# Two quarters of an output weight: split halves stored by one tile and loaded by the next, in a two-layer encoder kernel

## The chip, the cores and the metric

The kernel runs on one core of a Trainium2 chip. The metric is the device time of one execution in microseconds (us); the median of three runs is taken. The engines are TensorE (PE; its weight loads are PEld), VectorE (DVE), ScalarE (ACT), GpSimd (POOL) and SyncE (SP), which issues nearly all transfers.

## The reference

Two layers over 2048 rows of width 1024: a chunked gating mixer, then attention of chunks of 64 rows over a band of nine chunks, whose output is gated, multiplied by `w_out` (1024 x 1024) and added to the residual; a last norm ends it.

```python
def chunk_attention_mixer(h, k_pad, v_pad, w_qz, rel_bias, w_out):
    q, z = jnp.split(h @ w_qz, 2, axis=-1)
    ...
    def one_chunk(args):
        ...
        sc = jnp.einsum('bqhd,bkhd->bhqk', qc, kc).astype(jnp.float32) + bias
        sc = jnp.where(valid[None, None, None, :], sc, NEG_INF)
        p = jax.nn.softmax(sc, axis=-1).astype(vc.dtype)
        return jnp.einsum('bhqk,bkhd->bqhd', p, vc)
    ...
    return (o * jax.nn.silu(z)) @ w_out

def reference(x, ...):
    x = x + gmlp_mixer(rms_norm(x, a_norm_g[0]), ...)      # layer A
    k_pad, v_pad = shared_kv(x, kv_norm_g, w_kv)
    x = x + chunk_attention_mixer(rms_norm(x, b_norm_g[0]), k_pad, v_pad, ...)
    return rms_norm(x, final_norm_g)
```

## The kernel before

All products are made of three matmuls each (`mm3`, L110): a float32 operand is split into a high part, which is its conversion to the TensorE format by ScalarE, and a low part, which is the operand less the high part, by VectorE. `split_in` (L240) does this for a weight block of 128 x 1024: one conversion (L241) and one subtraction (L242).

Layer A and the values of all heads come first. What matters here is the attention layer, whose first load of values (`V`) is issued at 1521.4 us. It goes through four tiles `t` = 0 to 3 of 512 rows, and in each through eight pairs of heads `p`. In a pair, `score` makes the scores of a block of 128 rows (tiles `s`; VectorE takes bias and maximum into `pr`, `nm`; ScalarE the exponential; GpSimd the scaling), `flip` transposes them (`tp`) and splits the result into `pt` (ScalarE L1583, VectorE L1584), and `value` multiplies `pt` with the values (`pv`). There is one buffer each for `s` and for `tp`, so the next one waits until VectorE has read the last. Between these steps TensorE is given other matmuls: the projections of the next pair (`pj`) and the output product of the tile before (`bo`).

The output product of a tile is a Strassen scheme of seven phases in the order `PHS` = 1, 7, 2, 6, 5, 4, 3 with two row groups `jp` each, so 14 products of 12 matmuls. Phase `ph` takes a quarter of `w_out`, or a sum of quarters, as its right side, in two blocks `q` = 0, 1, each as a high and a low half. The right sides of phases 4 to 7 are sums: while tile 1 runs, `o_sums` makes and splits them and stores the halves in DRAM as `ows[ph, q]`; later tiles load the two halves (512 KB each). Phases 1, 2 and 3 take plain quarters (`o_raw`): each tile loads them raw (512 KB per block, tile `raw_bo`) and splits them. For tiles 0, 1 and 2 this is `o_right(t)` with the output product `outs[t]` run while tile t + 1 is attended to; the halves lie in the eight buffers of tag `T`, which the projection weights share. For the last tile it is `last_right(ph, q)`: phases 1, 7, 6 and 4 use tag `T` (`whbo`, `wlbo`), phase 2 the four buffers of tag `raw` (also `whbo`, `wlbo`), phase 5 a buffer of `V`, and phase 3 the one of `PT` (both `wbo`), which is free after the last `value`. The first 13 of its 56 steps run within the last head pair, the rest after it.

`last_open` loads the rest of the left side for the last tile into `A_hh`; `third` forms a difference of it on GpSimd. The rows of the results are called `row0` to `row3` in the last tile and `oc`, `ou` before; finished rows of the third tile are stored to `x2d`, loaded again as `y`, scaled (L1907) and stored to the output.

The program states the dependences; a scheduler puts each engine's instructions in an order, and each engine then works through its own in that order. `on_beat` ties an instruction behind the last transpose of the latest `flip`. An instruction that issues a transfer stands in the order of the engine that issues it, here SP, or ScalarE.

## Time and profile before

| What | Value |
|---|---|
| median of three runs | 2639.57 us (2638.92 to 2641.89) |
| profiled execution | 2640.17 us, its span 2638.1 us |
| granted TensorE clock, mean | 0.999 |
| data moved by transfers | 720.31 MB, mean 273 GB/s |
| 512 KB loads of raw output-weight blocks (`raw_bo`) | 24, 4.4 us to landing in the median |
| 512 KB loads of stored halves (`wh_bo`, `wl_bo`) | 24 each, 5.1 and 6.0 us |

The span is what the profiler saw from the first to the last instruction; the execution's own time lies 2.07 us above it. Times of instructions are counted from the span's start. In the rows of the profile the names have no numbers, so `wl_bo` stands for the low halves of all phases of tiles 0 to 2, and `wlbo` for those of the last tile.

### The profile page before, as it was taken

To read this page: it belongs to the slowest core of one execution; us is meant where nothing else is said; L and a number is where in the kernel's file an instruction comes from. 1 tells how busy PE (TensorE), PEld (TensorE's weight loads), DVE (VectorE), ACT (ScalarE), POOL (GpSimd) and SP (SyncE) were. 2 spreads that over 40 slices of the span, in tenths; PEclk is the share of its full clock that TensorE was granted. 3 is DMA by queue.
4 is the path that set the end of the run, shared out by engine and by line. 5 is a ranking of instruction groups with operands and counts; after the bars stand their busy time and mean duration, and the time that the engine had idled before them with its cause. 6 is when DMAs were issued, how large, how long until landed. Compare 5 with 4: busy or idle time off the path is not lost. (4 is left out here: it accounts for less than half of the span.)

```text
span 2638.1 us, 38018 instructions
## 1 busy us (share of the span) xinstructions
PE 2604.5 (99%) x12976; PEld 2177.8 (83%) x12976; DVE 1871.4 (71%) x2942; ACT 1314.7 (50%) x2331; POOL 890.1 (34%) x871
## 2 busy tenths in 40 slices
PE   9999999999999999999999999999999999999997
PEld 7888888788888888888888878888888888888886
DVE  6655676766667668757776767778778777877677
ACT  6422243443433434343466466666656655666564
POOL 4611335143252332203334334343333322332245
PEclk9999999999999999999999999999999999999999
DMA  7898998999988968968886587778787767775676
GB/s 299 316 345 332 347 364 319 315 327 328 333 302 303 331 224 310 342 205 262 322 279 234 184 277 236 233 244 260 248 278 253 228 208 222 252 228 162 192 229 249
DMA packets 275153, 720.31 MB, mean 273 GB/s; under 512 B 28944, under 2 KB 68880, under 8 KB 274960
## 3 DMA queue, kind: packets, MB, share of 16 engines
q1 hardware_dynamic: 268096, 704.25, 78.1%
q10 hardware_dynamic: 6864, 13.63, 1.4%
q8 instruction: 104, 1.70, 0.3%
q14 instruction: 89, 0.73, 0.1%
HBM read 532.69 MB, written 174.59 MB: 268 GB/s over the span
## 5 line engine op out<-in xcount | busy, mean ns | idle before, releaser
L111 PE MATMUL P<-T,S 128*128 128x512 f32 x1248 | 495.3, 397 | 0.0
L113 PE MATMUL P<-T,S 128*128 128x512 f32 x1248 | 487.6, 391 | 0.1
L112 PE MATMUL P<-T,S 128*128 128x512 f32 x1248 | 487.0, 390 | 0.0
L1563 POOL TENSOR_SCALAR pr<-pr,sl 128x640 f32<-128x640 f32 (+4 forms) x256 | 207.9, 812 | 554.1 <-DVE sl L1562 477.7
L111 PE MATMUL pj<-hh_b,wh_b 128*128 128x512 f32 x768 | 318.6, 415 | 0.0
L113 PE MATMUL pj<-hh_b,wl_b 128*128 128x512 f32 x768 | 304.0, 396 | 0.3 <-DVE wl_b L242 0.2
L112 PE MATMUL pj<-hl_b,wh_b 128*128 128x512 f32 x768 | 302.7, 394 | 0.0
L1559 ACT ACTIVATE pr<-pr,nm 128x640 f32<-128x640 f32 (+4 forms) x256 | 195.6, 764 | 198.8 <-DVE nm L1549 196.6
L113 PEld LDWEIGHTS P<-T,S 128*128 128x128 f32 x1248 | 234.3, 188 | 51.0 <-DVE S L463 0.4
L112 PEld LDWEIGHTS P<-T,S 128*128 128x128 f32 x1248 | 235.0, 188 | 44.7 <-DVE T L463 0.4
L111 PEld LDWEIGHTS P<-T,S 128*128 128x128 f32 x1248 | 234.7, 188 | 44.5 <-issue 0.2
L1584 DVE TENSOR_TENSOR pt<-tp,pt 128x640 fp32r<-128x640 f32 (+4 forms) x256 | 188.7, 737 | 48.9 <-ACT pt L1583 46.0
L1549 DVE CUSTOM_DVE_ANT_0 pr<-s,bias 128x640 f32<-128x640 f32 (+4 forms) x256 | 188.3, 736 | 43.8 <-PE s L1541 38.8
L1583 ACT CAST pt<-tp 128x640 fp32r<-128x640 f32 (+4 forms) x256 | 158.6, 619 | 38.5 <-PE tp L1579 32.6
L1579 PE MATMUL tp<-ident,pr 128*128 128x128 f32 x1120 | 166.5, 274 | 8.5 <-DVE pt L1584 7.4
L113 PEld LDWEIGHTS pj<-hh_b,wl_b 128*128 128x128 f32 x768 | 144.2, 188 | 34.5 <-DVE wl_b L242 2.3
L1579 PEld LDWEIGHTS tp<-ident,pr 128*128 128x128 f32 x1120 | 130.9, 140 | 42.5 <-issue 13.8
L111 PEld LDWEIGHTS pj<-hh_b,wh_b 128*128 128x128 f32 x768 | 145.1, 189 | 17.7 <-ACT wh_b L241 1.2
L1604 PEld LDWEIGHTS pv<-pt,V 128*128 128x128 f32 x896 | 142.8, 188 | 20.3 <-DVE pt L1584 3.4
L112 PEld LDWEIGHTS pj<-hl_b,wh_b 128*128 128x128 f32 x768 | 145.1, 189 | 16.5
L1604 PE MATMUL pv<-pt,V 128*128 128x256 f32 (+3 forms) x896 | 154.8, 320 | 0.8 <-ACT pt L1583 0.5
L242 DVE TENSOR_TENSOR wl_b<-raw_b,wh_b 128x1024 fp32r<-128x1024 f32 x96 | 121.0, 1261 | 25.1 <-ACT wh_b L241 22.9
(307 smaller groups left out, 5720.8 us busy)
## 6 DMA issues: line engine op xcount, KB each, us to landing
S<-hsd SPq DMA_DIRECT2D x288, 512.0 KB, 5.3
rw<-in_w_a SPq DMA_DIRECT2D x108, 512.0 KB, 6.2
raw_b<-wk SPq DMA_DIRECT2D x75, 512.0 KB, 4.5
A<-ytd SPq DMA_DIRECT2D x72, 512.0 KB, 5.7
hsd<-S SPq DMA_DIRECT2D x56, 512.0 KB, 4.9
V<-vhd SPq DMA_DIRECT2D x56, 512.0 KB, 5.6
bias<-reld SPq DMA_DIRECT2D x64, 320.0 KB, 4.0
va<-vd SPq DMA_DIRECT2D x32, 512.0 KB, 5.7
```

The lines of the kernel that those rows point to most:

```text
L111: first = mm(ps, lh, rh, start=first, stop=False)
L112: mm(ps, lh, rl, start=False, stop=False)
L113: mm(ps, ll, rh, start=False, stop=last)
L242: tv(wl[:], raw[:], wh[:].bitcast(F32), op=sub)
L1549: peak = nc.vector.tensor_tensor_reduce(out=pr[:, c0:].rearrange("p (a b) -> p a b", a=nseg), in0=ps[:, :nseg, :w], in1=bias[:, c0:].rearr ...
L1559: nc.scalar.activation(pr[:, c0:], pr[:, c0:], AF.Exp, scale=-1.0, bias=nm[:], accum_out=sl[:])
L1563: nc.gpsimd.tensor_scalar(pr[:, c0:], pr[:, c0:], sl[:], 1.0, op0=ALU.mult, op1=ALU.mult)
L1579: ins = tpose(tp[:, b, :], pr[:, b * P : (b + 1) * P], ident[:])
L1583: nc.scalar.copy(oh, tp[:, b0:5, :].rearrange("p a b -> p (a b)"))
L1584: nc.vector.tensor_tensor(pt[:, 2560 + o + b0 * P : 2560 + o + 640], tp[:, b0:5, :].rearrange("p a b -> p (a b)"), oh.bitcast(F32), op=ALU ...
L1604: mm(po[:, q0 * P : q1 * P], vtl[t, p][:, i, hs], rhs, start=(i == blocks[0] and j == 0), stop=(i == 7 and j == 1),)
```

## The change

The halves of phase 3 that `o_right(1)` splits (while the third tile, t = 2, is attended to) and those of phase 2 that `o_right(2)` splits (while the last tile is attended to) are put on a list `halves_out`. One entry of the list is stored to `ows` behind each `flip`, issued by ScalarE: 8 stores of 512 KB. The third tile's product then loads the halves of phase 3, and the last tile's product those of phases 2 and 3, as it does for phases 4 to 7. Each such block costs two loads of 512 KB where it was one load and a split. Six blocks of 128 x 1024 are concerned. Phase 1 is split as before.

```diff
     ows = {
         (ph, q): dram.tile([P, 2, 1024], F32, name=f"ows{ph}_{q}")
-        for ph in range(4, 8) for q in range(2)
+        for ph in range(2, 8) for q in range(2)
     }
...
                 w = [w_tile(f"w{i}_{name}") for i in "hl"]
-                if ph in o_raw:
+                if ph in o_raw and (t, ph) != (2, 3):
                     raw = raw_w(1, f"raw_{name}")
                     nc.sync.dma_start(raw[:], wb_out[o_raw[ph]][q])
                     hi = split_in(raw, *w)
                     if (ph, q) == (1, 1):
                         on_beat(hi)
+                    if (t, ph) in ((1, 3), (2, 2)):
+                        halves_out.extend(
+                            (ows[ph, q][:, i, :], w[i][:].bitcast(F32)) for i in range(2)
+                        )
                 else:
...
         owed_out = []
+        halves_out = []
...
                 w = [w_tile(f"w{i}{name}")[:] for i in "hl"]
-            if ph in o_raw:
+            if ph == 1:
                 raw = raw_w(NT - 1, f"raw_{name}")
...
                     send_all()
+                    if halves_out:
+                        on_beat(nc.scalar.dma_start(*halves_out.pop(0)))
                     square_all()
```

The scheduler's order moves with it, at the end of the program above all. In the names below, the digits behind a name are tile, phase and block or row group (`wl_bo2_3_0`: third tile, phase 3, block 0), the last tile's names have no tile number, and the last number counts the buffers.

VectorE, in the last tile while heads 13 and 14 are worked on, before (`Slo` are low halves of the left side, `pr`, `nm`, `sl` belong to the scores, `ou` are results of the third tile):

```order
L242 TENSOR_TENSOR wl_bo2_3_0_25169<-raw_bo2_3_0_25170,wh_bo2_3_0_25168 128x1024
L1562 RECIPROCAL sl3_14_1_25136<-sl3_14_1_25136 128x1
L1584 TENSOR_TENSOR pt3_13_25014<-tp3_13_3_25152,pt3_13_25014 128x640
L1957 TENSOR_TENSOR ou2_7_0_23262<-bo2_4_0_25141,ou2_7_0_23262 128x512
L242 TENSOR_TENSOR wl_bo2_3_1_25175<-raw_bo2_3_1_25176,wh_bo2_3_1_25174 128x1024
L1549 ISA pr3_14_2_25191,nm3_14_2_25192<-s3_14_2_25186,bias3_14_24925 128x640
L1549 ISA nm3_14_2_25192 128x1
L361 TENSOR_TENSOR Slo2_3_0_25239<-A2_01_23593,Sho2_3_0_25238 128x512
L1562 RECIPROCAL sl3_14_2_25193<-sl3_14_2_25193 128x1
L1626 TENSOR_TENSOR og32_3_6_25023<-pv3_13_25202,ot3_13_25228 64x512
L1584 TENSOR_TENSOR pt3_14_25219<-tp3_14_0_25220,pt3_14_25219 128x640
L1742 SCALAR_TENSOR_TENSOR A_hh_25180<-og32_3_6_25023,Z3_6_24702 128x256 x2
```

and now:

```order
L1566 RECIPROCAL sl3_14_1_25148<-sl3_14_1_25148 128x1
L1588 TENSOR_TENSOR pt3_13_25026<-tp3_13_3_25164,pt3_13_25026 128x640
L1962 TENSOR_TENSOR ou2_7_0_23270<-bo2_4_0_25153,ou2_7_0_23270 128x512
L1553 ISA pr3_14_2_25199,nm3_14_2_25200<-s3_14_2_25194,bias3_14_24937 128x640
L1553 ISA nm3_14_2_25200 128x1
L365 TENSOR_TENSOR Slo2_3_0_25247<-A2_01_23601,Sho2_3_0_25246 128x512
L1566 RECIPROCAL sl3_14_2_25201<-sl3_14_2_25201 128x1
L1630 TENSOR_TENSOR og32_3_6_25035<-pv3_13_25210,ot3_13_25236 64x512
L1747 SCALAR_TENSOR_TENSOR A_hh_25188<-og32_3_6_25035,Z3_6_24714 128x256 x2
L1588 TENSOR_TENSOR pt3_14_25227<-tp3_14_0_25228,pt3_14_25227 128x640
```

The two subtractions of phase 3 are gone, and the two `A_hh` now stand ahead of the first `pt3_14`.

SyncE, in the last 50 us of the program, before:

```order
L1897 DMA y2_0_1_25507<-x2d2_0_154 128x512
L1787 DMA whbo_6_0_25548<-ows6_0_106 128x1024
L1787 DMA wlbo_6_0_25549<-ows6_0_106 128x1024
L1787 DMA whbo_6_1_25552<-ows6_1_107 128x1024
L1787 DMA wlbo_6_1_25553<-ows6_1_107 128x1024
L1667 DMA out_0<-y2_0_0_25506 128x512
L1667 DMA out_0<-y2_0_1_25507 128x512
L1901 DMA y2_2_25581<-x2d2_2_156 128x1024
L1787 DMA wbo_5_1_25622<-ows5_1_105 128x1024 x2
L1795 DMA row3_25627<-x1d3_63 128x1024
L1787 DMA whbo_4_0_25648<-ows4_0_102 128x1024
L1787 DMA wlbo_4_0_25649<-ows4_0_102 128x1024
```

and now:

```order
L1902 DMA y2_0_1_25511<-x2d2_0_158 128x512
L1792 DMA wbo_5_0_25520<-ows5_0_108 128x1024 x2
L1792 DMA whbo_6_0_25552<-ows6_0_110 128x1024
L1792 DMA wlbo_6_0_25553<-ows6_0_110 128x1024
L1792 DMA whbo_6_1_25556<-ows6_1_111 128x1024
L1792 DMA wlbo_6_1_25557<-ows6_1_111 128x1024
L1672 DMA out_0<-y2_0_0_25510 128x512
L1672 DMA out_0<-y2_0_1_25511 128x512
L1906 DMA y2_2_25585<-x2d2_2_160 128x1024
L1792 DMA wbo_5_1_25626<-ows5_1_109 128x1024 x2
L1800 DMA row1_25629<-x1d3_63 128x1024
L1800 DMA row3_25631<-x1d3_63 128x1024
```

The two loads of `wbo_5_0` and that of `row1`, which stood some 15 to 20 rows further ahead, now stand here; behind these rows come the halves of phase 4 as before, and then four loads of `wbo_3_0` instead of the two raw ones.

VectorE, from the split of the left side of phase 3 in the last tile on, before:

```order
L361 TENSOR_TENSOR Qlo_3_0_25802<-A_hl_25181,Qho_3_0_25801 128x512
L1957 TENSOR_TENSOR row1_25625<-bo_4_0_25794,ou3_7_0_25586 128x512
L1784 TENSOR_TENSOR wbo_3_0_25678<-raw_bo_3_0_25679,wbo_3_0_25678 128x1024
L1784 TENSOR_TENSOR wbo_3_0_25678<-raw_bo_3_1_25683,wbo_3_0_25678 128x1024
L1889 TENSOR_TENSOR rr_f3_1_25814<-ssq3_1_25764 128x1
L361 TENSOR_TENSOR Qlo_3_1_25830<-A_hl_25181,Qho_3_1_25829 128x512
L125 TENSOR_SCALAR rr_f3_1_25814<-rr_f3_1_25814 128x1
L1957 TENSOR_TENSOR row3_25627<-bo_4_1_25822,ou3_7_1_25639 128x512
L1907 SCALAR_TENSOR_TENSOR row1_25625<-row1_25625,rr_f3_1_25814,gf_13667 128x512 x2
L1889 TENSOR_TENSOR rr_f3_3_25842<-ssq3_3_25788 128x1
```

and now:

```order
L365 TENSOR_TENSOR Qlo_3_0_25802<-A_hl_25189,Qho_3_0_25801 128x512
L365 TENSOR_TENSOR Qlo_3_1_25830<-A_hl_25189,Qho_3_1_25829 128x512
L1962 TENSOR_TENSOR row1_25629<-bo_4_0_25794,ou3_7_0_25590 128x512
L1962 TENSOR_TENSOR row3_25631<-bo_4_1_25822,ou3_7_1_25643 128x512
L1894 TENSOR_TENSOR rr_f3_1_25814<-ssq3_1_25764 128x1
L125 TENSOR_SCALAR rr_f3_1_25814<-rr_f3_1_25814 128x1
L1912 SCALAR_TENSOR_TENSOR row1_25629<-row1_25629,rr_f3_1_25814,gf_13671 128x512 x2
L1894 TENSOR_TENSOR rr_f3_3_25842<-ssq3_3_25788 128x1
L125 TENSOR_SCALAR rr_f3_3_25842<-rr_f3_3_25842 128x1
L1912 SCALAR_TENSOR_TENSOR row3_25631<-row3_25631,rr_f3_3_25842,gf_13671 128x512 x2
L1962 TENSOR_TENSOR row0_25560<-bo_3_0_25850,ou3_1_0_25488 128x512
```

The subtractions that made `wbo_3_0` are gone; rows 1 and 3 are scaled ahead of the addition of `row0`, which now stands right ahead of that of `row2`.

TensorE's last nine rows (before, the last twelve were all of `bo_3_1`) are now:

```order
L113 MATMUL bo_3_0_25850<-wbo_3_0_25682,Qlo_3_0_25802 128x512
L111 MATMUL bo_3_0_25850<-wbo_3_0_25682,Qho_3_0_25801 128x512
L112 MATMUL bo_3_0_25850<-wbo_3_0_25682,Qho_3_0_25801 128x512
L113 MATMUL bo_3_0_25850<-wbo_3_0_25682,Qlo_3_0_25802 128x512
L112 MATMUL bo_3_1_25874<-wbo_3_0_25682,Qho_3_1_25829 128x512
L113 MATMUL bo_3_1_25874<-wbo_3_0_25682,Qlo_3_1_25830 128x512
L111 MATMUL bo_3_1_25874<-wbo_3_0_25682,Qho_3_1_25829 128x512
L112 MATMUL bo_3_1_25874<-wbo_3_0_25682,Qho_3_1_25829 128x512
L113 MATMUL bo_3_1_25874<-wbo_3_0_25682,Qlo_3_1_25830 128x512
```

The two products of phase 3 are mixed now, and `bo_3_0` ends five matmuls ahead of the end.

## The prediction, made before the changed kernel ran

> **What bounds the kernel now.** I read the page's busy shares first, then the page's slices, then busy time by stretches for the last 80 us, then the order of time there. TensorE is busy nearly all the time, so a change elsewhere can pay only where TensorE idles.
>
> ```profile
> PE 2604.5 (99%) x12976; PEld 2177.8 (83%) x12976; DVE 1871.4 (71%) x2942; ACT 1314.7 (50%) x2331; POOL 890.1 (34%) x871
> ```
>
> The span is 2638.1 us, so 33.6 us are idle in all. The stretches show where the end loses (length; then PE, PEld, DVE, ACT, POOL busy; clock; DMA share; GB/s).
>
> ```profile
> 2558.00:2564.00 6.00, 5.76 (x35) 4.89 (x34) 5.15 (x10) 2.34 (x6) 2.87 (x4) 1.00 0.98 313
> 2564.00:2570.00 6.00, 5.10 (x25) 3.50 (x23) 6.00 (x12) 5.11 (x12) 3.56 (x3) 1.00 0.73 264
> 2570.00:2576.00 6.00, 4.56 (x27) 3.80 (x27) 6.00 (x10) 3.15 (x6) 4.07 (x5) 1.00 0.96 320
> 2576.00:2582.00 6.00, 5.54 (x30) 4.35 (x29) 6.00 (x13) 4.72 (x9) 2.46 (x3) 1.00 0.78 220
> 2582.00:2588.00 6.00, 4.92 (x30) 4.05 (x29) 6.00 (x7) 3.70 (x7) 5.68 (x6) 1.00 0.90 333
> 2588.00:2594.00 6.00, 4.42 (x23) 3.21 (x22) 4.53 (x12) 4.03 (x7) 1.32 (x2) 1.00 0.90 290
> 2594.00:2600.00 6.00, 6.00 (x34) 5.02 (x33) 3.45 (x7) 1.28 (x3) 0.55 (x1) 1.00 1.01 358
> 2600.00:2608.00 8.00, 8.00 (x37) 6.63 (x36) 6.39 (x11) 3.70 (x8) 4.40 (x4) 1.00 1.02 401
> 2621.00:2629.00 8.00, 6.73 (x28) 4.58 (x26) 7.27 (x12) 3.24 (x8) 3.80 (x4) 1.00 0.16 59
> 2629.00:2638.00 9.00, 0.00 (x0) 0.00 (x0) 5.28 (x11) 0.81 (x3) 1.10 (x2) 0.63 0.49 183
> ```
>
> From 2558 to 2594 TensorE idles 0.24 + 0.90 + 1.44 + 0.46 + 1.08 + 1.58 = 5.70 us, while VectorE is busy in every one of the 24 us from 2564 to 2588: there VectorE is the bound. From 2621 to 2629 another 1.27 us are idle, and the last 9 us hold no matmul. The transfers are near their limit too, from 2588 to 2608 above all. TensorE's own waits, in order of time (start, length, instruction, idle before it and what ended it):
>
> ```profile
> 2558.79 2.53 PE L1604 MATMUL pv<-pt,V 128*128 128x512 f32 x15 [0.24 <-DVE pt L1584]
> 2564.96 0.74 PE L1579 MATMUL tp<-ident,pr 128*128 128x128 f32 x5 [0.41 <-DVE pt L1584]
> 2567.57 0.56 PE L1541 MATMUL s<-K,Qh 128*128 128x320 f32 x2 [0.49 <-DVE nm L1549]
> 2570.92 0.74 PE L1579 MATMUL tp<-ident,pr 128*128 128x128 f32 x5 [0.91 <-DVE pt L1584]
> 2575.06 0.74 PE L1579 MATMUL tp<-ident,pr 128*128 128x128 f32 x5 [0.53 <-DVE pt L1584]
> 2577.90 0.50 PE L1604 MATMUL pv<-pt,V 128*128 128x512 f32 x1 [0.46 <-ACT pt L1583]
> 2586.04 0.74 PE L1579 MATMUL tp<-ident,pr 128*128 128x128 f32 x5 [1.08 <-DVE pt L1584]
> 2589.94 0.73 PE L1579 MATMUL tp<-ident,pr 128*128 128x128 f32 x5 [0.84 <-DVE rr_f L1889]
> 2593.69 0.74 PE L1579 MATMUL tp<-ident,pr 128*128 128x128 f32 x5 [0.73 <-DVE pt L1584]
> ```
>
> They add up to 5.69 us, and all but one are released by VectorE.
>
> **The change, part by part.** It removes six splits, each one conversion on ScalarE and one subtraction on VectorE: two of phase 3 in the third tile, two each of phases 2 and 3 in the last. All six lie in the last 85 us.
>
> *Phase 3 of the third tile.*
>
> ```profile
> 2555.62 2.32 DVE L242 TENSOR_TENSOR wl_bo<-raw_bo,wh_bo 128x1024 fp32r<-128x1024 f32 x1
> 2559.26 1.68 DVE L242 TENSOR_TENSOR wl_bo<-raw_bo,wh_bo 128x1024 fp32r<-128x1024 f32 x1
> 2560.86 0.81 DVE L1549 CUSTOM_DVE_ANT_0 pr<-s,bias 128x640 f32<-128x640 f32 x1
> 2555.22 3.87 POOL L1945 TENSOR_TENSOR ou<-ou,or 128x512 f32<-128x512 f32 x2
> L1784 DVE TENSOR_TENSOR wlbo<-raw_bo,whbo x4: 1209/1214/2085, 2568.8 to 2593.9; 128x1024 fp32r<-128x1024 f32 x4
> L1784 DVE TENSOR_TENSOR wbo<-raw_bo,wbo x2: 1710/2010/2309, 2620.8 to 2622.5; 128x1024 fp32r<-128x1024 f32 x2
> ```
>
> VectorE loses 2.32 + 1.68 = 4.00 us of work just ahead of its saturated stretch. The score's maximum that stands behind them (2560.86) can go at about 2558.1, and all that follows it in the queue with it. The last tile's two phase-2 subtractions (two of the four `wlbo`, at 1.21) give another 2.42 us. So 6.4 us of VectorE's work leave a stretch where TensorE waits 5.7 us for it. I followed the new order through with these durations, wait by wait. The waits of 0.24, 0.49, 0.91, 0.53, 1.08, 0.84 and 0.73 go or shrink to a tenth. The 0.46 goes for another reason: ScalarE's `pt` stood behind a conversion that is removed, and which itself sat waiting for its load:
>
> ```profile
> 2576.21 1.05 ACT L1783 CAST whbo<-raw_bo 128x1024 fp32r<-128x1024 f32 x1 [2.49 <-DMA raw_bo<-in_wb_out]
> 2563.99 0.82 DVE L1584 TENSOR_TENSOR pt<-tp,pt 128x640 fp32r<-128x640 f32 x1
> 2564.74 2.03 DVE L1742 SCALAR_TENSOR_TENSOR A_hh<-og,Z 128x256 f32<-128x256 f32 x2
> ```
>
> The 0.41 stays, since `pt` of the flip before now stands behind the two `A_hh` (2.03 us). A new wait of about 0.6 appears at a score whose maximum stands behind the two scalings of `y`. That leaves 5.28 - 1.0 = 4.3 us. The ends are 0 and 5.7; I take 3.9, near the upper end, because the freed work exceeds the wait by 0.7 us only.
>
> The first subtraction took 2.32 us beside a GpSimd addition and 1.21 us elsewhere. [...]
>
> *Phase 3 of the last tile.*
>
> ```profile
> 2621.53 0.39 PE L111 MATMUL bo<-wbo,Qho 128*128 128x512 f32 x1
> 2622.60 0.50 PE L112 MATMUL bo<-wbo,Qho 128*128 128x512 f32 x1 [0.69 <-DVE wbo L1784]
> 2624.84 0.50 PE L112 MATMUL bo<-wbo,Qho 128*128 128x512 f32 x1 [0.57 <-DVE wbo L1784]
> 2628.60 0.39 PE L113 MATMUL bo<-wbo,Qlo 128*128 128x512 f32 x1
> 2633.66 1.41 DVE L1907 SCALAR_TENSOR_TENSOR row<-row,rr_f,gf 128x512 f32<-128x512 f32 x2 [0.66 <-POOL rr_f L126]
> ```
>
> Here the wait is TensorE's own: 0.69 + 0.57 = 1.26 us go, if the halves have landed. Behind the last matmul (2629.0) the rows 1 and 3 no longer queue with row 0 and row 2, because the two subtractions of 1.71 and 2.31 us are gone from VectorE. Against that, the new order finishes row 0 only five matmuls before row 2. The tail of 9.1 us becomes about 8.7: 0.4, between 0 and 1.5.
>
> *Added transfers.* Six loads of 512 KB become twelve, and eight stores of 512 KB are issued by ScalarE.
>
> ```profile
> 2602.95 0.32 SPq L1787 DMA_DIRECT2D wlbo<-ows  x1
> wlbo<-ows SPq DMA_DIRECT2D x1, 512.0 KB, 10.4
> 2604.19 1.62 SPq L1782 DMA_DIRECT2D raw_bo<-in_wb_out  x2
> raw_bo<-in_wb_out SPq DMA_DIRECT2D x2, 512.0 KB, 10.5
> L1425 ACTq DMA_DIRECT2D vhd<-v x7: 366/367/379, 1494.0 to 1517.3; - x7
> 2260.00:2270.00 10.00, 9.18 (x49) 7.54 (x48) 8.14 (x18) 6.56 (x16) 6.00 (x9) 1.00 0.82 248
> ```
>
> Phase 4's last half, issued at 2602.95, lands at 2613.4, and the raw phase 3 by 2616.2. The order puts two loads of phase 5 and one `row` behind 2588 and adds two halves of phase 3, 2.6 MB; one raw phase-2 load (0.5 MB) leaves. 2.1 MB at 401 GB/s are 5.2 us, of which 1.2 us fit into the two stretches of 6 us with a DMA share of 0.90, so the last halves land at about 2620 if nothing starts earlier. Most of these loads are issued when buffers come free behind TensorE, which runs some 3 us earlier by then: about 2617. Phase 3 began at 2621.53, now some 3.9 us earlier; ten of its matmuls at 0.23 us use the first half, so the second is needed near 2619.9. The cover is 3 us. I charge 0.3 us; ends 0 and 3, the upper by the rate of 290 GB/s (2.1 MB in 7.2 us).
>
> [...]
>
> Eight issues at 0.37 us are 3.0 us of ScalarE, half of it around 2265 and half in the last tile's fourth head pair. ScalarE has 3.4 us free in the 10 us shown, so I charge 0.1, from -0.3 (other order of flips at the 0.82 us gap) to 1. In that stretch also six transposes and scores move by a matmul or two; nothing for that.
>
> **Sum.** 3.9 + 1.3 + 0.4 - 0.3 - 0.1 = 5.2 us. The profiled execution took 2640.17 us, 0.60 above the median of the three runs. Taken from the median, 2639.57 - 5.2 = 2634.4 us.
>
> **Rivals.**
> *The relief is mostly not cashed in*: VectorE's queue is in order and its instructions wait on ScalarE and GpSimd; or the late halves eat it. For it: TensorE needs the chain score, maximum, exponential, flip whatever VectorE has left. Against it: VectorE had no idle time for 24 us. The chain then gives a third, 1.5 + 1.3 - 0.7 = about 2 us: 2637.5.
> *GpSimd takes the turn*: of the 4.00 us only 2 x 1.21 are VectorE's own, and the additions that lay beside them (3.87 us for two) now delay other two-input work instead. The freed work is then 2.42 + 2.42 = 4.8 us against waits of 5.7, and the walked relief of 3.9 shrinks in proportion 4.8/6.4 to 2.9: 2635.4. [...] Against it: those additions end at 2559, and the next GpSimd additions come at other times.
> *All waits go and the tail shrinks too*: 5.7 + 1.27 + 1 = 8 us: 2631.6. Against it the `A_hh` order above.
> *Slower*: a store on ScalarE's queue holds everything behind it until an earlier transfer has landed, exponentials above all. The order shows that several of the eight wait for an earlier transfer. At landings of 4 to 5 us and some 1.5 us of free ScalarE per flip, a hold of 3.4 us costs 1.9 us, times eight 15 us, less 5.2: 2649. It decides from a hold of 2.8 us, where it outweighs the gain by 5.3. Against it: seven stores of the same size on that queue took 0.366 to 0.379 us each, none held.
> *The change does nothing*: not possible, since six splits are gone from the order.
>
> **How the numbers follow.** A measurement of this kernel tells about 0.2%, 5.3 us, from no change. Chances: the walked relief 0.45, all waits gone 0.09, GpSimd's turn 0.15, the relief mostly lost 0.22, slower 0.09. The first value lies almost on the bound: of it 0.35 falls beyond, of the second all, of the third 0.04. So faster 0.48, same 0.43, slower 0.09. The range goes from half a microsecond below all waits gone, 2631.0, to just above no change, 2640.5; the walked relief alone is 2632.5 to 2636.
>
> **What would show it.** Right: no subtraction of L242 at 2555 and none of phases 2 and 3 in the last tile; TensorE idle from 2558 to 2600 down from 5.7 to about 2 us; no wait for `wbo` by VectorE; last matmul near 2624. Wrong: TensorE waiting for transfers of `wbo`, `whbo` or `wh_bo` there; VectorE idle yet the transposes waiting for GpSimd or ScalarE; ScalarE held at a store.

## The result, and the profile after

The changed kernel took 2635.43 us in the median of 17 runs, the kernel before 2638.92 us in 17 runs beside it: a ratio of 0.9985, 95% interval 0.9979 to 0.9991. So the change gains 3.5 us where 5.2 were forecast, 2635.4 where 2634.4 were; in relative terms it lies within the 0.2% that the prediction set for no change. The gain was missed by 1.7 us, the time by 1.0 only: the forecast started from 2639.57 us, a median of three runs that lay 0.65 above the median of 17. That is luck. The profiled execution took 2636.53 us with a span of 2634.7, 3.4 us less than before.

The page's line of busy shares, and then the same stretches as before (length; PE, PEld, DVE, ACT, POOL busy; clock; DMA share; GB/s):

```profile
PE 2605.3 (99%) x12976; PEld 2180.3 (83%) x12976; DVE 1863.3 (71%) x2936; ACT 1309.8 (50%) x2325; POOL 885.7 (34%) x871
```

```profile
2558.00:2564.00 6.00, 6.00 (x37) 5.41 (x36) 4.09 (x10) 3.45 (x8) 2.37 (x3) 1.00 0.96 294
2564.00:2570.00 6.00, 6.00 (x34) 4.79 (x33) 6.00 (x13) 5.76 (x13) 1.59 (x2) 1.00 1.00 376
2570.00:2576.00 6.00, 5.00 (x26) 3.84 (x25) 5.57 (x6) 2.04 (x5) 6.00 (x5) 1.00 0.78 272
2576.00:2582.00 6.00, 4.16 (x18) 3.74 (x18) 5.68 (x14) 3.08 (x7) 3.71 (x5) 0.79 0.83 221
2582.00:2588.00 6.00, 6.00 (x35) 5.30 (x34) 4.30 (x10) 3.85 (x8) 4.47 (x6) 0.92 0.90 333
2588.00:2594.00 6.00, 6.00 (x32) 4.54 (x31) 4.83 (x9) 3.52 (x8) 1.99 (x3) 1.00 0.98 301
2616.00:2621.00 5.00, 5.00 (x23) 4.14 (x23) 4.62 (x8) 2.48 (x7) 4.33 (x4) 1.00 0.58 227
2621.00:2629.00 8.00, 4.05 (x18) 3.00 (x16) 5.83 (x12) 1.50 (x6) 1.59 (x3) 0.89 0.35 131
```

TensorE's idle time from 2558 to 2594 fell from 5.70 to 2.84 us, all of it in two waits where there were nine; TensorE waits neither for `wbo` nor for any transfer. The two waits, and the first and last of the rows by which the traces are compared below (the second piece of one `pv` in the last tile, and the last matmul):

```profile
2573.41 0.73 PE L1583 MATMUL tp<-ident,pr 128*128 128x128 f32 x5 [1.00 <-DVE pt L1588]
2578.07 0.56 PE L1545 MATMUL s<-K,Qh 128*128 128x320 f32 x2 [1.84 <-DVE nm L1553]
...
2524.49 1.67 PE L1608 MATMUL pv<-pt,V 128*128 128x512 f32 x9
2624.66 0.39 PE L113 MATMUL bo<-wbo,Qlo 128*128 128x512 f32 x1
```

What stands ahead of these two waits, on VectorE and GpSimd:

```profile
2568.41 3.52 POOL L1725 TENSOR_TENSOR A_hl<-A_hh 128x512 f32<-128x512 f32 x2 [6.78 <-DMA A_hh<-ogd]
2569.11 1.66 DVE L1789 TENSOR_TENSOR wlbo<-raw_bo,whbo 128x1024 fp32r<-128x1024 f32 x1
2570.70 1.77 DVE L365 TENSOR_TENSOR Qlo<-A_hh,Qho 128x512 fp32r<-128x512 f32 x1
2572.47 0.80 DVE L1588 TENSOR_TENSOR pt<-tp,pt 128x640 fp32r<-128x640 f32 x1
2573.64 1.28 POOL L1736 TENSOR_TENSOR A_hl<-A_hh 128x512 f32<-128x512 f32 x1
2573.70 2.98 DVE L1912 SCALAR_TENSOR_TENSOR y<-y,rr_f,gf 128x512 f32<-128x512 f32 x2 [0.43 <-POOL rr_f L126]
2577.20 0.81 DVE L1553 CUSTOM_DVE_ANT_0 pr<-s,bias 128x640 f32<-128x640 f32 x1
2585.83 1.50 DVE L1912 SCALAR_TENSOR_TENSOR y<-y,rr_f,gf 128x512 f32<-128x512 f32 x2
```

The maximum that TensorE waits for (2577.20) stands behind two scalings of `y` that waited 0.43 us for their root and then took 2.98 us beside GpSimd; the next pair took 1.50. In the kernel before the same two scalings took 2.56 us, and the last of the four subtractions for `wlbo` came only behind TensorE's last wait (2593.69):

```profile
2574.84 2.56 DVE L1907 SCALAR_TENSOR_TENSOR y<-y,rr_f,gf 128x512 f32<-128x512 f32 x2
2593.93 1.22 DVE L1784 TENSOR_TENSOR wlbo<-raw_bo,whbo 128x1024 fp32r<-128x1024 f32 x1
```

And the end: the additions that finish the rows (L1962) and their scalings (L1912):

```profile
2619.04 1.37 DVE L1962 TENSOR_TENSOR row<-bo,ou 128x512 f32<-128x512 f32 x2
2621.53 1.41 DVE L1912 SCALAR_TENSOR_TENSOR row<-row,rr_f,gf 128x512 f32<-128x512 f32 x2 [0.67 <-POOL rr_f L126]
2623.86 1.42 DVE L1912 SCALAR_TENSOR_TENSOR row<-row,rr_f,gf 128x512 f32<-128x512 f32 x2 [0.66 <-POOL rr_f L126]
2625.19 1.28 DVE L1962 TENSOR_TENSOR row<-bo,ou 128x512 f32<-128x512 f32 x2
2627.74 1.42 DVE L1912 SCALAR_TENSOR_TENSOR row<-row,rr_f,gf 128x512 f32<-128x512 f32 x2 [0.66 <-POOL rr_f L126]
2630.07 1.42 DVE L1912 SCALAR_TENSOR_TENSOR row<-row,rr_f,gf 128x512 f32<-128x512 f32 x2 [0.66 <-POOL rr_f L126]
```

The last matmul ends at 2625.05, 3.94 us earlier than before, but 9.7 us follow it where there were 9.1.

**How the traces are compared.** Whole runs of one kernel scatter (the 17 of the kernel before go from 2635.31 to 2644.99 us), and much of that arises far ahead of the change: in the fourteen traces the `pv` shown above begins anywhere from 2520.75 to 2528.21. So I count from that `pv` (2523.84 before) to the end of the last matmul, and from there to the end of the span. Each kernel has one trace, so differences of a few tenths there carry no weight, and where the medians say otherwise, they decide. The medians are of 11 runs (the kernel with middle and end mended: 5; the kernel before and the changed one: 17), the ratios against runs of the kernel before beside them.

| Kernel | to the last matmul | behind it | sum | against before | median, us | ratio (95% interval) |
|---|---|---|---|---|---|---|
| before | 105.15 | 9.1 | 114.3 | | 2638.92 | |
| changed | 100.56 | 9.7 | 110.3 | -4.0 | 2635.43 | 0.9985 (0.9979 to 0.9991) |
| stores only | 105.54 | 9.1 | 114.7 | +0.4 | 2641.06 | 1.0006 (0.9998 to 1.0015) |
| third tile only | 103.89 | 9.1 | 113.0 | -1.3 | 2638.34 | 0.9995 (0.9987 to 1.0004) |
| last tile, phase 2 only | 103.40 | 9.1 | 112.5 | -1.8 | 2636.64 | 0.9993 (0.9984 to 1.0002) |
| last tile, phase 3 only | 103.27 | 11.3 | 114.6 | +0.3 | 2639.04 | 1.0000 (0.9992 to 1.0009) |
| changed, end reordered once | 100.21 | 9.7 | 109.9 | -4.4 | 2635.87 | 0.9987 (0.9978 to 0.9996) |
| changed, one `y` later | 99.48 | 10.2 | 109.7 | -4.6 | 2635.94 | 0.9985 (0.9977 to 0.9994) |
| both of these | 98.73 | 10.3 | 109.0 | -5.3 | 2636.60 | 0.9991 (0.9982 to 1.0000) |
| changed, `third` on VectorE | 100.83 | 9.5 | 110.3 | -3.9 | 2636.84 | 0.9989 (0.9981 to 0.9998) |
| changed, end mended | 101.24 | 8.5 | 109.7 | -4.6 | 2635.95 | 0.9989 (0.9980 to 0.9998) |
| changed, middle and end mended | 97.36 | 8.7 | 106.1 | -8.2 | 2630.49 | 0.9966 (0.9954 to 0.9979) |
| the same, phase 1 too | 99.30 | 10.6 | 109.9 | -4.4 | 2640.53 | 1.0007 (0.9998 to 1.0016) |
| before, middle and end mended | 103.72 | 9.1 | 112.85 | -1.4 | 2638.13 | 0.9997 (0.9988 to 1.0006) |

### The profile page after: what moved, and what is told of

It is laid out like the page before. It is cut to its first block, busy times and chain, and to the rows that moved or that the text cites. A ratio compares the mean times of both kernels' runs of the same rounds, so it can differ in the third digit from the quotient of the medians.

```text
span 2634.7 us, 38034 instructions
## 1 busy us (share of the span) xinstructions
PE 2605.3 (99%) x12976; PEld 2180.3 (83%) x12976; DVE 1863.3 (71%) x2936; ACT 1309.8 (50%) x2325; POOL 885.7 (34%) x871
```

## Experiments: the parts of the change, one at a time

The diffs show only the lines that matter, with comments for the reader.

**The stores alone.** The kernel before, with the stores added:

```diff
+                    if (t, ph) in ((1, 3), (2, 2)):
+                        halves_out.extend(...)      # stored by ScalarE, loaded by nobody
```

> The kernel before with the eight stores by ScalarE added; nobody loads what they store, all six splits stay. Theory of the ledger (the change's cost lies in the stores: flips in the fourth head pair come two matmuls later, TensorE's place in the program is 0.4 to 0.6 us later at 2500): about 0.5 us slower than before, span 2638.6, TensorE idle from 2558 to 2600 unchanged at 5.7 us. Rival (the stores cost nothing, the 0.6 us come from the loads of the changed kernel): 0.0 us, TensorE's place at 2500 as before within 0.2 us. Second rival (a store holds ScalarE): a store of more than 0.5 us on ScalarE's queue and several us slower.

From another `pv`, at 2253, to the one at 2524 it took 271.43 us against 270.83 before and 271.29 in the changed kernel, so 0.5 to 0.6 us are lost there; behind 2524 another 0.4. No store was held: each issue took 0.33 to 0.34 us, here and in the changed kernel, whose rows are these (min, median, max in ns; first and last start):

```profile
L2080 ACTq DMA_DIRECT2D ows<-wh_bo x4: 326/332/343, 2260.5 to 2421.1; - x4
L2080 ACTq DMA_DIRECT2D ows<-wl_bo x4: 326/326/338, 2261.3 to 2426.8; - x4
```

Of the loss, 0.4 us arise at one place: at 2421.9 and 2426.0 two flips follow the matmul ahead of them by 0.41 and 0.40 us, two matmuls later in the program than before; a stop too short for the list of waits. From one `pv` at 2416 to one at 2432 all ten kernels that store phase 2's halves there lose 0.38 to 0.42 us against before, and the three others lose nothing. So the loss is in the order that the stores bring.

**The third tile alone.** Only `o_right(2)` loads its halves of phase 3.

```diff
-                    if (t, ph) in ((1, 3), (2, 2)):
+                    if (t, ph) == (1, 3):
...
-            if ph == 1:
+            if ph in o_raw:
```

> Only the third tile's phase 3 loads its halves (four stores, phase 3 alone); the last tile splits phases 2 and 3 as before. Additive theory (VectorE is the bound from 2558 to 2594, each us taken off it is worth the same): 4.0 of the 6.4 us go, so 4.0/6.4 of the 3.4 us that the stretch gave, 2.1 us, less 0.3 for four stores: about 1.8 us faster; TensorE idle from 2558 to 2600 down from 5.7 to about 3.6 us; the two waits of 0.69 and 0.57 us for wbo stay. Saturating theory (the chain score, maximum, exponential, flip bounds as soon as some work is gone): about 3 us faster, idle down to about 2.9 as in the changed kernel. GpSimd's turn (of the 4.0 us only 2.4 were VectorE's own): about 1.0 us faster, idle about 4.4 us.

**The last tile's phase 2 alone.** The third tile and the last tile's phase 3 split as before (`(t, ph) == (2, 2)` stores, `ph in (1, 3)` splits).

> Only the last tile's phase 2 loads its halves (four stores, phase 2 alone); phase 3 is split by the third and the last tile as before. Additive theory: 2.4 of the 6.4 us go, 1.3 us, less 0.2 for the stores: about 1.1 us faster, TensorE idle from 2558 to 2600 about 4.4 us, waits for wbo of 1.26 us stay. Saturating theory: 2 to 3 us faster, idle about 3 us. GpSimd's turn: the 2.4 us are half of VectorE's own 4.8 us, 1.7 us faster, idle about 4.0.

**The last tile's phase 3 alone.** (`(t, ph) == (1, 3)` stores, `ph in (1, 2)` splits in the last tile, the third tile splits.)

> Only the last tile's phase 3 loads its halves (four stores, phase 3 alone); the third tile splits phase 3 and the last tile phase 2 as before. Additive theory: the two waits of 0.69 and 0.57 us go (1.1 us by TensorE's place), the time behind the last matmul grows from 9.1 to about 9.6 us, 0.3 for the stores: about 0.3 us faster; TensorE idle from 2558 to 2600 stays at about 5.7. Theory of the prediction for this term: 1.3 + 0.4 - 0.3 = 1.4 us faster, time behind the last matmul about 8.7 us. Rival: the halves land late, TensorE waits for a transfer of wbo: no faster or slower than before.

To the last matmul the three parts gain 1.26, 1.75 and 1.88 us, 4.89 in all, and the whole change 4.59: they add up, and the saturating theory is out. But the additive theory's price, the same for each us taken off VectorE, fails too: 4.0 us of subtractions were worth 1.26 us and 2.4 us were worth 1.75. The idle sums that I had forecast were wrong as well: 5.28 and 4.56 us stayed for the first two, where 3.6 and 4.4 were expected. What fell was the number of stops, nine before, five and seven here (below, on the hardware). By size GpSimd's turn did better than the additive theory: it had 1.0 and 1.7 us for these two parts, the additive one 1.8 and 1.1. With one trace each, and medians whose intervals include no gain, this does not settle it; the runs with a mended order below speak to it.

The third part is the telling one. TensorE's waits for `wbo` are gone, the last matmul comes 1.88 us earlier (all of it within phase 3; up to there the trace differs from that of before by 0.03 us), and the span ends no earlier, because 11.3 us follow instead of 9.1. Its VectorE rows at the end:

```profile
2634.51 1.42 DVE L1912 SCALAR_TENSOR_TENSOR row<-row,rr_f,gf 128x512 f32<-128x512 f32 x2 [0.66 <-POOL rr_f L126]
2635.84 0.68 DVE L1962 TENSOR_TENSOR row<-bo,ou 128x512 f32<-128x512 f32 x1
2638.39 1.42 DVE L1912 SCALAR_TENSOR_TENSOR row<-row,rr_f,gf 128x512 f32<-128x512 f32 x2 [0.66 <-POOL rr_f L126]
```

The last row's addition starts at 2635.84, 4.4 us behind the last matmul (2631.48), because it stands behind the scalings of the row before. Here the end is a chain on VectorE, and TensorE's gain in phase 3 is worth nothing in it; the median (2639.04 us, ratio 1.0000) says the same.

## Experiments: VectorE's order

**The end, reordered once.** The last product is kept behind the one before it on TensorE, row 0's scalings behind row 2's addition.

```diff
+                    if (ph, jp, k) == (3, 1, 0):
+                        follow(ins, ended)          # the last matmul of the product before
...
-                if last:
+                if last and b == 0:
+                    held_scale.append(scale)        # released by row 2's addition, behind it
```

> The changed kernel, with the last product of phase 3 kept behind the one before it on TensorE, and row 2's addition kept ahead of row 0's two scalings on VectorE. Theory (the tail grew by 0.55 us because row 0 finishes only a few matmuls before row 2, so row 2's chain queues behind row 0's on VectorE): row 0's sum starts near 2.7 us before the last matmul ends, row 2's chain runs unhindered, the time behind the last matmul falls from 9.65 to about 7.9 us; about 1.7 us faster than the changed kernel, 5 us faster than before. Rival (the tail is the chain of one row and its store, whatever the order): 9 to 9.7 us, no gain. Second rival (the second half of phase 3 has not landed when the first product wants it alone): TensorE waits for wbo, the last matmul ends up to 1 us later.

The rival held: 9.7 us behind the last matmul. Row 0's addition did not come earlier, since it stands behind the scalings of row 3, which the edit had left alone.

**One `y` later.** Row 1's scaling of the third tile goes behind the next score's maximum.

```diff
+                    if (t, b) == (NT - 2, 1):
+                        finals[:0] = [lambda: late.append(scale)]   # run behind the next score
```

> The changed kernel, with the scaling of y of the third tile's row 1 kept behind the next score's maximum on VectorE; nothing else is asked for. Theory (the new wait of 1.84 us is VectorE's order: two scalings of 2.98 us together stand ahead of a maximum that TensorE waits for): that wait falls to under 0.5 us, TensorE idle from 2558 to 2600 falls from 2.84 to about 1.3, about 1.5 us faster than the changed kernel. Rival (the chain bounds; another instruction takes its place): idle stays at 2.3 us or more, under 0.5 us gained.

**Both edits together.**

> Both of the edits of the two runs before it, in one kernel. If both theories hold, and the two places lie apart in time: 1.7 + 1.5 = 3.2 us faster than the changed kernel, about 6.5 us faster than before, ratio 0.9975. If the relief is eaten at the end because the last loads land no earlier: TensorE waits for a transfer of wbo, 1.5 to 2 us faster than the changed kernel.

The wait of 1.84 us went, and with it 1.1 us (the first) and 1.8 us (both) up to the last matmul. But the expected fall in idle time did not come: a wait of 1.90 and 1.95 us appeared further on, at a flip whose `pt` now stood behind the scaling of row 3's `y`. That scaling was not only long. VectorE came to it before its `y` had landed and stood still for 1.32 us, as the row of the first kernel shows (with both edits for 1.08, where the profile names GpSimd's `A_hl`):

```profile
2586.71 1.69 DVE L1913 SCALAR_TENSOR_TENSOR y<-y,rr_f,gf 128x512 f32<-128x512 f32 x2 [1.32 <-DMA y<-x2d]
```

The load was issued at 2580.16 and took 6.5 us. The first theory was right on the place and the rival on the replacement. Both edits together did not bring the 3.2 us forecast over the changed kernel: 1.3 by the trace, and by the runs nothing (2636.60 us, ratio 0.9991, where the changed kernel has 0.9985).

**`third` on VectorE.** The two subtractions that GpSimd did in 3.52 us.

```diff
-                    on_beat(tg(la["s3"][:, cs], la["00"][:, cs], la["10"][:, cs], op=sub))
+                    on_beat(tv(la["s3"][:, cs], la["00"][:, cs], la["10"][:, cs], op=sub))
```

> The changed kernel, with the two subtractions of 128x512 that GpSimd did in 3.52 us from 2568.4 given to VectorE. Theory (VectorE and GpSimd take turns where both read two operands from SBUF): the subtraction for wlbo falls from 1.66 to about 1.2 us, the Qlo from 1.77 to about 0.7, GpSimd's scaling of pr from 1.24 to 0.8, and the two subtractions take about 0.7 us each on VectorE, so VectorE gains 1.5 and loses 1.4 us and TensorE's idle time from 2558 to 2600 stays within 0.7 us of 2.84. Rival (these instructions are long for another reason, such as the transfers into SBUF): they keep 1.6 to 1.8 us, VectorE has 1.4 us more to do, TensorE idles about 4.2 us and the kernel is about 1.4 us slower than the changed one.

Its rows:

```profile
2569.38 1.35 DVE L1725 TENSOR_TENSOR A_hl<-A_hh 128x512 f32<-128x512 f32 x2
2570.76 1.30 POOL L1736 TENSOR_TENSOR A_hl<-A_hh 128x512 f32<-128x512 f32 x1 [0.22 <-DMA A_hh<-ogd]
2571.40 1.74 DVE L1789 TENSOR_TENSOR wlbo<-raw_bo,whbo 128x1024 fp32r<-128x1024 f32 x1
2573.13 0.67 DVE L365 TENSOR_TENSOR Qlo<-A_hh,Qho 128x512 fp32r<-128x512 f32 x1
```

The Qlo fell from 1.77 to 0.67 us and the two subtractions cost 0.68 each. The one for `wlbo` stayed long (1.74), but GpSimd's next subtraction had moved up beside it. So the Qlo was long because of GpSimd, not of transfers: the DMA share was 0.94 over its 1.77 us (2570.7 to 2572.5 in the changed kernel) and 0.95 over the 0.67 here (2572 to 2574). In the changed kernel's rows `pt` and the maximum, which read PSUM, keep 0.80 and 0.81 us beside GpSimd. What grew beside GpSimd's subtractions has both inputs in SBUF: `wlbo` took 1.66 and 1.74 us where the one at 2566.39 in the changed kernel took 1.22, and the Qlo 1.77 against 0.67. GpSimd's own pair took 3.52 us; a single subtraction of that size took 1.29 at 2582.61, where VectorE was idle for most of it. Idle time from 2558 to 2600 was 2.48 us, and the sum is within 0.1 us of the changed kernel's. That does not price the turns: the wait for the maximum fell from 1.84 to 0.67 us and the flip's 1.00 went, but 1.51 us came at 2589.27, behind row 3's scaling, which had stood still for 1.44 us until its load landed at 2585.9, and 1.25 us at 2602.0, for ScalarE's `Qho`.

**The middle and the end mended.** Row 1's `y` behind the next maximum, row 3's behind the next flip; at the end, row 3's scalings behind row 0's addition and row 0's behind row 2's root.

```diff
+                    if t + 2 == NT and b % 2:
+                        finals[:0] = [lambda: late[b].append(scale)]  # 1: behind the next score, 3: the next flip
...
+                        if t + 2 == NT:
+                            follow(ins, peaks[-1:] + subs[-1:])
...
+                    if last and (ph, jp) == (3, 0):
+                        held_scale.pop()[1]([added])                  # row 3's scalings
...
+                    if b == 2:
+                        held_scale.pop(0)[1]([first.ins.name])        # row 0's, then row 2's
+                        held_scale.pop()[1]()
```

> The changed kernel with two orders mended. In the middle: row 1's y is scaled behind the next score's maximum and row 3's y behind the next flip's second half, so that neither stands ahead of what TensorE waits for. At the end: the last product of phase 3 stays behind the one before it, row 0's addition goes ahead of row 3's scalings, and row 2's root ahead of row 0's. Theory (both losses are VectorE's order): TensorE idle from 2558 to 2600 falls from 2.84 to under 1.3 us, no stretch at half the granted clock before the last matmul, last matmul 3 to 3.5 us earlier than in the changed kernel counted from the same matmul near 2524; time behind it 9.65 to about 7.8 us; together 4.5 to 5.5 us faster than the changed kernel, ratio to before 0.9965 to 0.9970. Rival 1 (a transfer bounds next: the DMA share is 1.0 from 2588 to 2616 in the changed kernel): TensorE waits for wbo or whbo at the end, only 1.5 to 3 us faster than the changed kernel. Rival 2 (row 3's y lands too late wherever it is scaled, and holds VectorE's queue): a wait of 1.5 us or more stays near 2587, 2.5 to 3.5 us faster.

It came nearly as the theory had it: 2630.49 us in the median of five runs, 0.9966 of the kernel before (0.9954 to 0.9979), where the changed kernel has 0.9985. TensorE's waits up to the last matmul, three of its stretches, and the first row's addition, the last row's, and the last scalings:

```profile
2573.44 0.73 PE L1583 MATMUL tp<-ident,pr 128*128 128x128 f32 x5 [0.22 <-DVE pt L1588]
2577.43 2.56 PE L1608 MATMUL pv<-pt,V 128*128 128x512 f32 x15 [0.28 <-DVE pt L1588]
2588.78 0.74 PE L1583 MATMUL tp<-ident,pr 128*128 128x128 f32 x5 [0.31 <-DVE pt L1588]
```

```profile
2570.00:2576.00 6.00, 5.78 (x31) 4.61 (x31) 6.00 (x10) 4.04 (x9) 6.00 (x5) 1.00 0.90 321
2576.00:2582.00 6.00, 5.72 (x34) 4.83 (x34) 5.64 (x13) 2.82 (x7) 4.44 (x6) 1.00 0.85 234
2616.00:2621.00 5.00, 5.00 (x23) 4.14 (x23) 4.07 (x10) 1.34 (x4) 2.55 (x4) 1.00 0.26 98
```

```profile
2574.56 2.08 DVE L1918 SCALAR_TENSOR_TENSOR y<-y,rr_f,gf 128x512 f32<-128x512 f32 x2
2616.67 1.28 DVE L1979 TENSOR_TENSOR row<-bo,ou 128x512 f32<-128x512 f32 x2
2623.08 0.68 DVE L1979 TENSOR_TENSOR row<-bo,ou 128x512 f32<-128x512 f32 x1
2626.60 1.41 DVE L1918 SCALAR_TENSOR_TENSOR row<-row,rr_f,gf 128x512 f32<-128x512 f32 x2 [0.44 <-POOL rr_f L126]
```

Idle time is 0.81 us, and GpSimd is as busy as in the changed kernel; row 1's scalings still take 2.08 us beside it. What is different is that the maximum stands ahead of them; the `pt` behind them costs TensorE 0.28 us. Of the end, 1.0 of the expected 1.85 us came: row 2's root still waited for the first half of row 0's scalings and took 0.99 us on GpSimd instead of 0.55. TensorE waits for no transfer (the DMA share is 0.26 ahead of 2621), so the first rival is out. The second is near: VectorE waits 0.34 us for row 3's `y` at 2585.87.

**The same orders without the change.** Both edits on the kernel before.

> The kernel before, with only the two mended orders of VectorE (and the last product of phase 3 behind the one before it); all six splits stay, nothing is stored by ScalarE. It tells what the change itself is worth once the orders are right. Theory (VectorE is saturated from 2564 to 2588 in the kernel before, so that order alone frees little there; the end still waits for the two splits of phase 3): TensorE idle from 2558 to 2600 between 3.5 and 5.5 us, the waits of 1.26 us for wbo stay, 1 to 3 us faster than before, so the change is worth 5 to 7 us on top. Rival (the orders were the whole loss, the splits only stood beside it): 7 to 8.5 us faster than before, as the changed kernel with both orders, and the change is worth nothing then.

By the trace 1.4 us, by the runs none that is certain. TensorE's idle time from 2558 to 2600 is 5.0 us, so order alone frees little where VectorE is full. One thing was wrong: the waits for `wbo` did not stay, two waits of 0.52 and 1.30 us for ScalarE's `Qho` near 2600 came in their place. With the orders mended the change is worth 112.85 - 106.1 = 6.8 us by the traces, as against 4.0 with its own; by the ratios, 0.9997 and 0.9966, it is worth about 8 us.

**Phase 1 too.** Phase 1's halves stored by the third tile's product and loaded by the last tile (four more stores).

```diff
-                    if (t, ph) in ((1, 3), (2, 2)):
+                    if (t, ph) in ((1, 3), (2, 2), (2, 1)):
...
-            if ph == 1:
+            if ph == 0:                               # never: the last tile splits nothing
```

> The same, and phase 1's halves too are stored by the third tile and loaded by the last one: two more subtractions (1.22 and 1.66 us in the changed kernel) and two conversions leave VectorE and ScalarE in the stretch, 1.0 MB more is loaded there. Theory (VectorE's work is still the bound there): another 0.5 to 1.5 us off TensorE's idle time. Rival (the transfers are the bound: the halves of phase 1 have to land in a stretch with a DMA share of 0.8 to 0.9): TensorE waits for a transfer of whbo near 2575, 1 to 3 us slower than the kernel without this part.

It gave all of it back: 2640.53 us. TensorE's largest wait, what VectorE waited for ahead of it, and a wait further on:

```profile
2350.28 0.79 PE L113 MATMUL pj<-hh_b,wl_b 128*128 128x512 f32 x1 [2.32 <-DVE wl_b L242]
2349.00 1.23 DVE L242 TENSOR_TENSOR wl_b<-raw_b,wh_b 128x1024 fp32r<-128x1024 f32 x1 [3.81 <-DMA ows<-wl_bo]
2578.52 0.50 PE L112 MATMUL bo<-wlbo,Qho 128*128 128x512 f32 x1 [0.74 <-DMA wlbo<-ows]
```

From 2253 to 2524 it took 276.7 us against 271.0 without this part, though it splits the same there. Projection weights and these halves share the buffers of tag `T`, and a half that is stored holds its buffer longer: VectorE stood still for 3.81 us until the store of a `wl_bo`, issued at 2342.37, had landed, and only then split the next projection weight. TensorE waited 2.32 us for it, 1.03 us for a later one at 2361.4, and the granted clock was 0.50 from 2350.07 to 2353.49. That is most of the loss. The rest lies behind 2524: 1.9 us up to the last matmul, where at 2578 the rival shows as well, a wait for a transfer, at 0.74 us smaller than feared, and 1.9 us behind it.

**The end's order alone.** The end as mended, the middle as in the changed kernel.

> The changed kernel with the second mended order alone, that at the end; up to the last products its order is the changed kernel's. Two questions. The end: the time behind the last matmul is 8.7 us as with both orders mended, 0.9 us less than in the changed kernel, if that gain belongs to the end's order alone; 9.6 us if it came from the middle. The middle: the waits of about 1.0 and 1.84 us near 2573 and 2578 come again. If the half granted clock behind them always follows a wait of that length in this order, the matmuls from 2579 to 2583 run at 0.50 here too; if it depends on when the wait falls, as the two waits of 1.82 to 1.95 us without it in other runs suggest, it may be absent, and the last matmul, counted from the same one near 2524, is then 1.5 us earlier than in the changed kernel (99.0 against 100.6 us).

Behind the last matmul 8.5 us: that gain belongs to the end's order alone. The waits came again (0.77 and 1.87 us) and the clock stayed at 1.00, but the last matmul was not 1.5 us earlier. It was 0.7 us later, with two more waits of 1.47 and 0.65 us for VectorE's `pt` at 2584.6 and 2590.4. Ahead of each VectorE had stood still at a scaling of `y` until its load had landed: 1.21 us for row 3's, issued at 2574.99 and 6.6 us on its way, and 1.10 us for a later one (2588.82). Of the stretch at half clock see the last section.

## Why the prediction was right and wrong

**VectorE's relief (3.9, ends 0 to 5.7).** The mechanism is right: VectorE bounds the stretch, and the removed subtractions free it. This is the term that was mis-sized most: it is 3.0 us by the two experiments of its parts (1.26 + 1.75), and 2.7 by the changed kernel less the part of phase 3. Two steps of its working do not hold on their own rows. "6.4 us of VectorE's work leave a stretch where TensorE waits" counts the second phase-2 subtraction, which began at 2593.93, behind the last of these waits; 5.2 us stood ahead of one. And "5.28 - 1.0" takes off the 0.41 twice, since 5.28 is already the sum without it: the walk gives 4.7, and the 3.9 was a choice below it.

The walk had left 1.0 us of waits: 0.41 at a flip, and "about 0.6" at a score whose maximum stands behind the two scalings of `y`. That second wait is the one found, at 1.84 us. The scalings took 2.98 us (2.56 before) and began 0.43 us late, behind a root from GpSimd. The 0.41 did not stay: the two `A_hh`, taken at 2.03 us, took 0.76. A wait of 1.00 us came at another flip instead, behind a `wlbo` of 1.66 us and a Qlo of 1.77. The step that failed is to follow the new order through "with these durations", those of the kernel before. In these traces the length of an instruction of VectorE with both inputs in SBUF depends on what GpSimd does beside it (the Qlo took 1.77 us beside GpSimd's pair of subtractions and 0.67 where VectorE did that pair), and the new order moves that: these three cost 0.44 + 1.09 + 1.48 = 3.0 us more than short rows of the same trace (1.22, 0.68, 1.50).

**GpSimd's turn** had 2635.4 as its time, which is what was measured, but not for its reason. It let the relief shrink in proportion to the freed work, to 2.9 us, which is near the 2.7 to 3.0 measured. But with the order mended GpSimd was as busy, a scaling pair was still long (2.08 us), and 105.15 - 97.36 = 7.8 us came up to the last matmul, 5.9 without phase 3's part (on the kernel before, the order alone gave 1.4). So the turns do not cap the relief at 2.9 us. What cost the time is the long instruction standing ahead of one that TensorE waits for; how much of the missing 1.2 us is due to the turns and how much to the order alone is not told apart.

**Phase 3 of the last tile (1.3).** The 1.26 us of waits went, and 1.88 us up to the last matmul where this part was done alone. The halves had landed.

**The end behind the last matmul (+0.4, ends 0 to 1.5).** Wrong in sign: 0.5 us longer, and the 8.7 us that it forecast came only when the order was mended. The step that failed is "the rows 1 and 3 no longer queue with row 0 and row 2". They do: row 0's addition at 2625.19 stands behind row 3's scalings of 2623.86. From row 1's addition to the end of the span it takes 15.7 us in the changed kernel and in both kernels with the end reordered once, and 14.6 in both with the end mended. Part of TensorE's gain in phase 3 is lost in that chain, all of it in the part done alone.

**Transfers (-0.3).** In the changed kernel nothing that TensorE needs waited for one: zero. TensorE did not wait for one in the fastest kernel either, where phase 3 begins 2.5 us earlier (2616.96 and 2619.45). But the loads are close: in three other orders VectorE stood still for 1.2 to 1.4 us until row 3's `y` had landed, and TensorE behind it.

**Stores (-0.1).** No store was held, so the slower rival had no case. But they move flips: 0.5 to 1.0 us, against the 0.1 charged. "Nothing for that" was the wrong step; two stops of some 0.2 us each are in the trace.

In the sum: 4.6 up to the last matmul, less 0.5 behind it and less 0.5 ahead of 2524, is 3.6; the medians give 3.5. That the forecast came this near is in part luck: relief, end and stores fell 1.2, 0.9 and 0.4 us short, while phase 3 and the transfers came out 0.6 and 0.3 better.

## What to carry to other kernels

When an engine that bounds is relieved, look in its new order for the first long instruction that now stands ahead of one the next engine waits for, and price it by what stands beside it there, not by its row in the old order (the Qlo took 1.77 us beside GpSimd's pair of subtractions, 0.67 where VectorE did that pair). Check as well that its own inputs will have landed by then (in three other orders VectorE stood still for 1.2 to 1.4 us until a `y` had landed). A gain of TensorE counts only as far as the chain behind its last matmul lets it (phase 3 alone: 1.88 us earlier, then 11.3 us instead of 9.1); walk that chain row by row in VectorE's order. Here mending these two orders raised the worth of the same change from 4.0 to 6.8 us by the traces.

## What the hardware showed

**Half the clock after some waits.** Every one of the fourteen traces has the same wait of 2.05 us of TensorE near 49 us. In seven of them the granted clock then falls to half for some 3.4 us, in seven it does not. Before and changed kernel, the wait and the stretches around it:

```profile
49.13 1.16 PE L637 MATMUL t<-ident,hb 128*128 128x128 f32 x8 [2.05 <-DVE S L463]
48.00:52.00 4.00, 2.87 (x17) 2.42 (x18) 3.37 (x6) 0.59 (x1) 3.38 (x3) 1.00 0.71 272
52.00:56.00 4.00, 4.00 (x22) 3.31 (x20) 0.69 (x1) 0.59 (x1) 0.47 (x1) 1.00 0.99 330
```

```profile
49.19 1.17 PE L641 MATMUL t<-ident,hb 128*128 128x128 f32 x8 [2.05 <-DVE S L467]
48.00:52.00 4.00, 2.81 (x13) 2.35 (x14) 3.43 (x6) 0.59 (x1) 3.32 (x3) 0.78 0.70 270
52.00:56.00 4.00, 4.00 (x16) 3.19 (x15) 0.69 (x1) 0.59 (x1) 0.51 (x1) 0.80 0.98 315
...
2576.00:2580.00 4.00, 2.16 (x11) 1.74 (x10) 4.00 (x10) 2.16 (x5) 2.14 (x3) 0.94 0.87 249
2580.00:2584.00 4.00, 4.00 (x22) 3.96 (x21) 2.10 (x6) 1.88 (x4) 3.56 (x5) 0.64 0.87 250
```

After the wait of 1.84 us it came too (2579.5 to 2582.9 at 0.50), and after that of 1.82 us in the kernel with the end reordered once; after waits of 1.82, 1.87, 1.90 and 1.95 us in four other kernels it did not. In all, from 10 us to the last matmul, the fourteen traces have 24 waits of TensorE above 1.7 us (1.78 to 2.32) and 11 such stretches, each of 3.4 us and each beginning from 0.24 us before to 1.42 us behind the end of one of these waits. None lies at a shorter wait, though there are some of up to 1.66 us. So 13 of the 24 had none, at lengths like those that had one; what decides between them is not shown by these runs. The stretch at 2579 cost nothing that these traces show. TensorE's order is the same up to the mixed products of phase 3 in three kernels: without the stretch the last matmul came after 101.24 us, with it after 100.56 and 100.21. At half clock TensorE, and VectorE behind it, came to row 3's `y` when it had landed; without it VectorE stood still there and at a later scaling for 1.21 and 1.10 us, as said above, and TensorE waited 2.1 us more for it.

**A stop costs more than the idle time listed.** Where phase 3 was loaded alone, two stops of 1.26 us in all went and the last matmul came 1.88 us earlier: 0.3 us a stop on top. The rows of the prediction show half of it: the matmul behind the wait of 0.69 us started 1.07 us after the one ahead, where 0.23 is usual, so 0.84 us were lost; the next one (2622.94) came 0.34 us on, which is another 0.11. Sums of idle time rank stretches, but the number of stops has to be counted in.
